# Attention of a two-layer diffusion transformer on one core: transposes and values issued in longer runs, three engines in an order written by hand, and a feed-forward entry without GpSimd

## The chip, the core and the metric

The kernel runs on one core of a Trainium2 chip. The metric is the device time of one execution in microseconds (us). Each engine of the core takes its instructions in the order in which they stand in its queue: PE (TensorE) multiplies matrices and transposes, DVE (VectorE) and ACT (ScalarE) do elementwise work and read PE's results out of PSUM, POOL (GpSimd) does elementwise work in SBUF, SP (SyncE) issues most DMAs. They wait for each other through semaphores.

## What is computed

Two post-norm layers over 1024 latent tokens with a prefix of 256 context tokens, model width 1024, all in float32. Layer 0 has two kinds of attention beside each other, layer 1 has one; each layer ends with a convolutional feed-forward network (FFN). Cut to what matters here:

```python
# layer 0, head group A: 8 query heads, 2 key heads, every latent query reads all 1280 keys
p = jax.nn.softmax(gqa_scores(q, k_all), axis=-1); y = gqa_out(p, v_all)
# layer 0, head group B: 8 heads, a neighbourhood of the grid with a bias, plus 256 context keys
p = jax.nn.softmax(jnp.concatenate([s_nb + bias, s_ctx], -1), axis=-1)
# layer 1: 16 query heads, 2 key heads, window of +-128 tokens, 256 context keys, one sink logit per head
p = jax.nn.softmax(jnp.concatenate([s_loc, s_ctx, sink_q], -1), axis=-1)
# every layer
x = layer_norm(ALPHA * x + gate * (y @ w_out), g, b)
f = (silu(conv(h @ w_up)[gate half]) * conv(h @ w_up)[value half]) @ w_down
x = layer_norm(ALPHA * x + gate * f, g, b)
```

## The kernel before

The program is one straight line without loops on the chip: projections of layer 0 (to about 316 us of the span), attention A (316 to 590), attention B (590 to 708), output projection, FFN of the context, FFN of the latents (to about 1650), projections of layer 1, attention C (1824 to 2067), output projection, FFN of layer 1 (from about 2170 to the end).

**A unit of attention.** Scores are computed for one block of 128 queries at a time. `qk_pair` (L911) multiplies q and k in float32r, three products for each of two heads, which PE runs on two halves of its rows; they land in a PSUM tile S of two banks, of which there are two buffers. DVE reads S, negates it, adds mask or bias and finds the row's minimum in the same instruction (L1177 and L1160 in A, L1315 and L1295 in B, L2947 in C; a further small one, L1182, joins two minima in A). `smax1` then has ACT compute the exponential with its sum (L934), DVE the reciprocal of the sum (L936), and POOL the product with it (L937). The result P has to be transposed for the product with v: PE transposes blocks of 128x128 against an identity (L1044 in layer 0, L1009 in layer 1), four to a PSUM bank T, of which there are three buffers; ACT or DVE copies a full bank to SBUF as PT (`evict`, L918, L922, L924); PE multiplies PT with v into the PSUM tile pv (L1058, L1018). In the profile each of these matmuls with v counts as two. One such bank, from its transposes to its products with v, is what the code calls a bank; its products are a closure called `late`.

**What sets the order.** `pipeline` walks over a list of slices. Each slice computes the scores of one unit (A takes three slices for a block of four heads: context keys, then the latent keys of two heads, then of the other two; B takes one slice for two heads of a block; C takes two slices of two heads). After the scores of a slice it issues the products with v of the banks that were transposed in the slice before (`flush`), and then transposes some more banks from a queue (`take`). On PE the order of each slice is therefore scores, values, transposes. The context manager `manual_pe` keeps the order in which the code is written for PE alone; the instructions of ACT, DVE, POOL and SP are placed by a scheduler of the compiler layer.

**Buffers.** The tile pv has one buffer of a PSUM bank, written anew for each block. P has 8 buffers in layer 0 and 12 in layer 1, PT 9 and 10. The queries of A are loaded into a pool of their own (`aq`, three buffers). Weights of the large products are split into a high and a low float32r part and kept in a ring of 12 SBUF buffers (`ring`).

**Work that goes along.** During B the first rows of the output weight are loaded into P buffers and split (`out_weight`, `split_out`, L1388 and L1389: a cast on ACT, a subtraction on DVE); in C it is the same with four pieces, and x is loaded, scaled and stored in eight groups (`x_load`, `x_scale`, L2890 to L2893).

**The entry of layer 1's FFN.** The last block of tokens runs through LayerNorm, is transposed and modulated (`build_B1`) and split into high and low parts (L1796, L1797). The sums of a Strassen scheme, tiles T0 to T3, are split in the same way by `make` (L1911 on ACT, L1912 on DVE or POOL), in three pieces each. Then PE's products L1879 of the first pair of FFN columns follow, in the order T1, T0, T2, T3. The subtraction of the last block's h3lb and the first, large piece of T0, T2 and T3 stand on POOL.

Of the kernel before, what the change touches and what calls it, by code (L numbers as in the profile page):

```python
# [29 lines left out]
NEG = -1e30  # L30
ORDER = [f + h for f in range(NF // 4) for h in (0, NF // 4)]
# [6 lines left out]
class Kern:  # L38
# [476 lines left out]
    def l0_project(self):  # L515
# [311 lines left out]
        self.aq = eA.enter_context(self.pool("aq", bufs=3))  # L827
# [64 lines left out]
    def load_q(self, qp, src):  # L892

        q = self.t(qp, [128, 2, 2, 256], "q", R)
        for j in range(2):
            self.nc.sync.dma_start(f32(q[:, j]), src[j])
        return q
# [28 lines left out]
    def smax1(self, sp, P, n, negm, nsink=None):  # L926

        nc = self.nc
        den = self.t(sp, [128, 1], "den", bufs=6)
        m = n  # L930
        if nsink is not None:
            nc.gpsimd.tensor_copy(P[:, n : n + 1], nsink)
            m = n + 1
        nc.scalar.activation(P[:, :m], P[:, :m], AF.Exp, bias=negm, scale=-1.0, accum_out=den)  # L934
        rin = self.t(sp, [128, 1], "rin", bufs=6)
        nc.vector.reciprocal(rin, den)  # L936
        nc.gpsimd.tensor_scalar(P[:, :n], P[:, :n], rin, 1.0, ALU.mult, ALU.mult)  # L937

    def pipeline(self, slices):

        fifo, late, pend = [], [], []

        def flush(n):
            done = False
            while len(late) > n and not (done and late[0][0]):
                done = late[0][1]  # L950
                late.pop(0)[3]()

        def take(pop, chunk, keep):
            flush(keep)
            n = 0
            while fifo and pop > 0:
                if n >= chunk:
                    flush(keep)
                    n = 0
                w, first, last, bank = fifo.pop(0)  # L960
                while sum(x[2] for x in late) + w > 9:
                    late.pop(0)[3]()
                late.append((first, last, w, bank()))
                pop -= w
                n += w

        for loads, unit, pop, banks, chunk, keep, *delay in slices:
            for ld in loads:
                ld()
            unit()  # L970
            take(pop, chunk, keep)
            fifo += pend
            pend = []
            if delay:
                pend = banks()
            else:
                fifo += banks()
# [2351 lines left out]
```

## Time and profile before

| | |
|---|---|
| time, median of 3 runs | 2816.75 us (2812.15 to 2818.3) |
| the profiled execution | 2817.18 us, span 2815.3 us |
| mean granted TensorE clock | 0.992 |
| busy share of the span | PE 97%, weight loads 80%, DVE 76%, ACT 49%, POOL 23% |
| chain that ended last | PE 70%, issue 10%, DVE 9%, DMA 4%, ACT 3%, POOL 2% |

The span is the time from the first to the last instruction; the execution takes 1.9 us more. A row of the timeline gives the start in us from the span's start, the duration of the merged group, engine, line, operation, names, shape, the number of instructions and in brackets the idle time of the engine before it with what ended it. The duration of a group of matmuls reaches to the modelled end of its last one; how long a group holds PE is read from its start to the start of the next group. A busy PE need not be at its peak.

### The profile page before, as it was taken

To read this page: it belongs to the slowest core of one execution; us is meant where nothing else is said; L and a number is where in the kernel's file an instruction comes from. 1 tells how busy PE (TensorE), PEld (TensorE's weight loads), DVE (VectorE), ACT (ScalarE), POOL (GpSimd) and SP (SyncE) were. 2 spreads that over 40 slices of the span, in tenths; PEclk is the share of its full clock that TensorE was granted. 3 is DMA by queue.
4 is the path that set the end of the run, shared out by engine and by line. 5 is a ranking of instruction groups with operands and counts; after the bars stand their busy time and mean duration, and the time that the engine had idled before them with its cause. 6 is when DMAs were issued, how large, how long until landed. Compare 5 with 4: busy or idle time off the path is not lost.

```text
span 2815.3 us, 45394 instructions
## 1 busy us (share of the span) xinstructions
PE 2739.8 (97%) x16724; PEld 2245.4 (80%) x16724; DVE 2147.6 (76%) x3867; ACT 1381.5 (49%) x2596; POOL 657.7 (23%) x953
## 2 busy tenths in 40 slices
PE   8999899999999999999999999999999999999998
PEld 6877677878889988888888888766677788888887
DVE  4886476776688778888877656677778888888878
ACT  4321355577336654555553344167754455455542
POOL 3601233355440000000001002255534111111002
PEclk9999999999999999999999999999999999999999
DMA  7669601042658653343367525652245355455962
GB/s 272 192 206 291 199 28 35 11 164 91 186 161 256 206 158 105 113 122 110 117 222 275 179 98 169 205 163 79 90 130 187 119 175 178 161 172 202 341 231 97
DMA packets 369349, 457.01 MB, mean 162 GB/s; under 512 B 26008, under 2 KB 265016, under 8 KB 367592
## 3 DMA queue, kind: packets, MB, share of 16 engines
q1 hardware_dynamic: 341512, 369.27, 41.2%
q0 software_dynamic: 24576, 82.89, 8.6%
q8 instruction: 131, 2.15, 0.3%
q10 hardware_dynamic: 3040, 1.97, 0.2%
q14 instruction: 90, 0.74, 0.1%
HBM read 338.11 MB, written 115.93 MB: 161 GB/s over the span
## 4 chain that ended last, share of the span: by engine, by line
PE 70%; issue 10%; DVE 9%; DMA 4%; ACT 3%; POOL 2%; SPq 0%; ACTq 0%; DVEq 0%; POOLq 0%
PE q L1879 7%; PE x L1879 7%; PE y L1879 6%; PE S L911 5%; PE dy L2585 4%; PE T L1044 4%; PE pv L1058 4%; PE mm L430 3%; PE v L1879 3%; PE mm L432 3%; PE mm L431 3%; PE dx L2585 3%; PE d L431 3%; PE d L432 3%; PE d L430 3%
## 5 line engine op out<-in xcount | busy, mean ns | idle before, releaser
L937 POOL TENSOR_SCALAR P<-P,rin 128x640 f32<-128x640 f32 (+3 forms) x288 | 252.1, 882 | 306.3 <-DVE rin L936 275.5
L1853 DVE TENSOR_TENSOR w<-raw,w 128x512 fp32r<-128x512 f32 x308 | 207.4, 687 | 84.1 <-ACT w L1851 83.7
L112 ACT CAST w<-raw 128x512 fp32r<-128x512 f32 x315 | 183.4, 621 | 167.9 <-PE d L432 64.6
L113 DVE TENSOR_TENSOR w<-raw,w 128x512 fp32r<-128x512 f32 x315 | 206.0, 695 | 69.5 <-ACT w L112 67.5
L911 PE MATMUL S<-k,q 64*128 64x256 f32 (+2 forms) x1824 | 198.4, 340 | 11.4 <-DVE nm L2947 4.4
L934 ACT ACTIVATE P<-P,nm 128x641 f32<-128x641 f32 (+4 forms) x208 | 161.4, 777 | 86.1 <-DVE nm L2947 46.4
L1851 ACT CAST w<-raw 128x512 fp32r<-128x512 f32 x308 | 182.2, 620 | 22.6 <-DVE raw L1858 11.3
L911 PEld LDWEIGHTS S<-k,q 64*128 64x128 f32 x1824 | 139.3, 190 | 49.6 <-issue 16.0
L1044 PE MATMUL T<-ident,P 128*128 128x128 f32 x1008 | 136.7, 283 | 12.0 <-POOL P L937 4.7
L430 PE MATMUL d<-w,w 128*128 128x512 f32 x352 | 137.5, 391 | 0.0
L432 PE MATMUL d<-w,w 128*128 128x512 f32 x352 | 137.0, 389 | 0.0
L431 PE MATMUL d<-w,w 128*128 128x512 f32 x352 | 137.0, 389 | 0.0
L1044 PEld LDWEIGHTS T<-ident,P 128*128 128x128 f32 x1008 | 110.5, 143 | 32.2 <-issue 17.9
L1058 PE MATMUL pv<-PT,v 128*64 128x128 f32 x2016 | 131.8, 279 | 3.7 <-ACT PT L924 2.5
L1058 PEld LDWEIGHTS pv<-PT,v 128*64 128x64 f32 x2016 | 109.0, 137 | 28.5 <-issue 13.5
L1879 PE MATMUL q<-T3h,w 128*128 128x512 f32 x352 | 118.7, 399 | 9.1 <-DVE ug L2539 7.1
L934 ACT ACTIVATE P<-P,mc 128x1280 f32<-128x1280 f32 (+1 forms) x80 | 94.7, 1188 | 64.5 <-DVE mc L1182 62.5
L936 DVE RECIPROCAL rin<-den 128x1 f32<-128x1 f32 x288 | 46.2, 161 | 100.1 <-ACT P L934 98.3
L2585 PE MATMUL dy<-w,w 128*128 128x512 f32 x528 | 120.8, 390 | 0.4 <-DVE w L113 0.4
L1879 PE MATMUL q<-T2h,w 128*128 128x512 f32 x352 | 115.8, 390 | 0.9 <-ACT q L2101 0.9
L2585 PEld LDWEIGHTS dy<-w,w 128*128 128x128 f32 x528 | 99.0, 188 | 21.8 <-DVE w L113 0.8
L1879 PE MATMUL y<-T1h,w 128*128 128x512 f32 x352 | 115.5, 389 | 0.0
(468 smaller groups left out, 7792.6 us busy)
## 6 DMA issues: line engine op xcount, KB each, us to landing
raw<-in_up_dram SPq DMA_DIRECT2D x132, 512.0 KB
raw<-in_down_dram SPq DMA_DIRECT2D x59, 512.0 KB
raw<-g SPq DMA_DIRECT2D x44, 512.0 KB
raw<-G SPq DMA_DIRECT2D x38, 512.0 KB
araw<-in_ada_w_dram SPq DMA_DIRECT2D x32, 512.0 KB
raw<-in_w_in_dram SPq DMA_DIRECT2D x28, 512.0 KB
g<-cv POOLq DMA_DIRECT2D x22, 512.0 KB, 3.0
G<-go POOLq DMA_DIRECT2D x44, 256.0 KB, 3.0
```

The lines of the kernel that those rows point to most:

```text
L113: (lo_eng or nc.vector).tensor_sub(lo, s, f32(hi))
L430: nc.tensor.matmul(ps, lh, rh, start=first, stop=False)
L431: nc.tensor.matmul(ps, lh, rl, start=False, stop=False)
L432: nc.tensor.matmul(ps, ll, rh, start=False, stop=last)
L911: self.nc.tensor.matmul(outs[a], q[r, x, qs], k[r, y, ks], start=(i == 0), stop=(i == 2))
L934: nc.scalar.activation(P[:, :m], P[:, :m], AF.Exp, bias=negm, scale=-1.0, accum_out=den)
L937: nc.gpsimd.tensor_scalar(P[:, :n], P[:, :n], rin, 1.0, ALU.mult, ALU.mult)
L1044: nc.tensor.transpose(ps[:, s * 128 : (s + 1) * 128], P[a][:, cols[i + x] : cols[i + x] + 128], self.ident,)
L1058: nc.tensor.matmul(O[a * HD : (a + 1) * HD], v_of(a, vts[i + x]), pT[:, s * 128 : (s + 1) * 128], start=(i + x == 0), stop=(i + x == m - 1 ...
L1853: nc.vector.tensor_sub(half(i, 1), src[i], f32(half(i, 0)))
L1879: nc.tensor.matmul(ps, w[:, a, s], r[b][:, k], start=first and k + i == 0, stop=k == 3 and i == 2, skip_group_check=True,)
L2585: nc.tensor.matmul(banks[q][t], ga[i][:, a, c], wd[i][:, b], start=q < 2 and f + k == 0, stop=f == HF - 1 and k == 2, skip_group_check=True,)
```

## The change

**Order.** `pipeline` is rewritten. A unit now returns its DVE reductions and its exponentials as two lists instead of issuing them. For each slice the code says how many banks to transpose and how many waiting products with v to keep back, so that a slice either transposes (up to ten banks in a row) or multiplies with v, not both. The new context manager `manual_all` fixes the written order on PE, ACT and DVE; POOL and SP stay with the scheduler. Reciprocals of one slice's sums are placed between the reductions of the next slice. In a slice that transposes, the exponentials stand behind the copies of the transposed banks; in one that does not, they stand ahead of the products with v. Which of ACT and DVE copies a bank out is a fixed string per stage ("AADAD" in C, ENGA in A, "AAA" and "DDA" by turns in B; A is ACT, D is DVE).

**Buffers.** The tile pv is allocated once and its two halves are used by turns (`o_half`). P in layer 0 has 7 buffers, and A has 4 of its own beside them; PT has 10; the queries of A are loaded into the ring. The small y tiles have 2 buffers where they had 3.

**Splits.** The output weight's pieces and the first block of the attention's result are split one slice (B) or one group (C) after their load is issued. The scaling of x follows one group after its load. In the FFN of the context, the split of the first row of the down weight moves from the end of the output projection into the first turn of the loop.

**FFN entry of layer 1.** The four subtractions on POOL move to DVE.

```diff
+ENGA = ("ADADA", "AADAD")
...
+        for loads, unit, keep, pop, banks in slices:
             for ld in loads:
                 ld()
-            unit()
-            take(pop, chunk, keep)
-            fifo += pend
...
+            reds, exps = unit()
+            for i, red in enumerate(reds):
+                red()
+                for f in fins[i * len(fins) // len(reds) : (i + 1) * len(fins) // len(reds)]:
+                    f()
+            n = min(max(pop(len(fifo)), 0), cap)
+            if not n:
+                fins = [e() for e in exps]
+            if keep is not None:
+                flush(keep)
+            flush(max(cap - n, 0))
+            for _ in range(n):
+                late.append(fifo.pop(0)())
+            if n:
+                fins = [e() for e in exps]
+            fifo += banks()
...
+    def o_half(self, O):
+        self.noh = getattr(self, "noh", -1) + 1
+        return O[:, self.noh % 2 * 256 : self.noh % 2 * 256 + 256]
...
+    def manual_all(self):
+        E = mybir.EngineType
+        return self.tc.manual_schedule(engines={E.PE, E.Activation, E.DVE})
...
-                        (ctx_part, 2, lambda: [], 4, 1),
-                        (lambda: lat_part(0), 5, lambda: banks(0), 5, 1),
-                        (lambda: lat_part(1), 3, lambda: banks(1), 4, 0),
+                        (ctx_part, 2 if t < 2 else None, (lambda n: 0) if (kv, t) == (0, 0) else (lambda n: n - 5), lambda: []),
+                        (lambda: lat_part(0), 4, (lambda n: n) if (kv, t) == (0, 0) else (lambda n: 0), lambda: banks(0)),
+                        (lambda: lat_part(1), 0, lambda n: 0, lambda: banks(1)),
...
-                        (unit(0), 3, lambda: [], 4, 0), (unit(1), 2, values, 4, 0)
+                        (unit(0), None if one else 0, lambda n: n if one else 0, lambda: []),
+                        (unit(1), 0 if one else None, lambda n: 0 if one else n, values),
...
-            (nc.gpsimd if t == NLAT - 1 else nc.vector).tensor_sub(l, s, f32(h))
+            nc.vector.tensor_sub(l, s, f32(h))
...
                 for m in (1, 0, 2, 3):
-                    make[m](0, eng=nc.gpsimd if m != 1 else None)
-                    make[m](1, 2)
+                    make[m](0, 1, 2)
```

What this does to the order shows best in pieces of the engines' queues. In the names, S is a score tile, T a bank of transposes, PT its copy, pv the product with v; a number behind a name tells tiles apart. PE in attention C before, from the end of one slice's scores to the next slice's transposes:

```order
L911 MATMUL S_19990<-k_18639,q_19711 128x384
L911 MATMUL S_19989<-k_18639,q_19711 128x384
L911 MATMUL S_19990<-k_18639,q_19711 128x384
L1018 MATMUL pv_19092<-PT_19972,v_19267 64x256 x2
L1018 MATMUL pv_19092<-PT_19979,v_19267 64x256 x2
L1018 MATMUL pv_19092<-PT_19986,v_19267 64x256 x2
L1009 MATMUL T_20025<-ident_58,P_19839 128x128
L1009 MATMUL T_20025<-ident_58,P_19897 128x128
```

And now, from the end of a slice's scores to the start of the next:

```order
L914 MATMUL S_19881<-k_18600,q_19660 128x384
L914 MATMUL S_19882<-k_18600,q_19660 128x384
L1023 MATMUL pv_19053<-PT_19844,v_19227 64x256 x2
L1023 MATMUL pv_19053<-PT_19851,v_19227 64x256 x2
L1023 MATMUL pv_19053<-PT_19858,v_19227 64x256 x2
L1023 MATMUL pv_19053<-PT_19865,v_19227 64x256 x2
L914 MATMUL S_19922<-k_18600,q_19660 128x256
L914 MATMUL S_19923<-k_18600,q_19660 128x256
```

Before, three (or two) banks' products with v stand between the scores and two or three banks of transposes. Now all the banks of a group stand in one run, and a run of scores follows each run of either kind.

ACT in attention A before; P is the exponential, den its sum, PT<-T the copy of a bank:

```order
L934 ACTIVATE P_4531,den_4660<-P_4531,mc_4527 128x1280
L934 ACTIVATE P_4532,den_4667<-P_4532,mc_4527 128x1280
L918 COPY PT_4718<-T_4713 128x512
L918 COPY PT_4767<-T_4762 128x512
L918 COPY PT_4810<-T_4805 128x512
L918 COPY PT_4817<-T_4812 128x512
L934 ACTIVATE P_4725,den_4785<-P_4725,mc_4723 128x1280
L934 ACTIVATE P_4726,den_4792<-P_4726,mc_4723 128x1280
L918 COPY PT_4838<-T_4833 128x512
L934 ACTIVATE P_4727,den_4856<-P_4727,mc_4723 128x1280
L934 ACTIVATE P_4728,den_4863<-P_4728,mc_4723 128x1280
```

And now, over one block of four heads:

```order
L921 COPY PT_4470<-T_4465 128x512
L921 COPY PT_4477<-T_4472 128x512
L921 COPY PT_4491<-T_4486 128x512
L921 COPY PT_4505<-T_4500 128x512
L921 COPY PT_4519<-T_4514 128x512
L921 COPY PT_4533<-T_4528 128x512
L938 ACTIVATE P_4438,den_4553<-P_4438,mc_4436 128x1280
L938 ACTIVATE P_4439,den_4555<-P_4439,mc_4436 128x1280
L938 ACTIVATE P_4440,den_4608<-P_4440,mc_4436 128x1280
L938 ACTIVATE P_4441,den_4610<-P_4441,mc_4436 128x1280
```

The copies stood between the exponentials, one to four at a time; now six copies follow each other, and the four exponentials of the block stand together ahead of the next six.

DVE at the entry of layer 1's FFN before, where the large pieces of T0, T2 and T3 and h3lbl are missing since they stand on POOL:

```order
L1812 TENSOR_TENSOR w_23606<-hst_23589,b_23480 128x512
L1796 CAST h3lbh_22676<-hst_23599 128x4x128
L1813 TENSOR_TENSOR w_23606<-hst_23599,w_23606 128x512
L1814 TENSOR_TENSOR w_23607<-hst_23599,hst_23589 128x512
L1815 TENSOR_TENSOR w_23607<-b_23492,w_23606 128x512
L1912 TENSOR_TENSOR T1l_23659<-gk_23660,T1h_23658 128x2x4x128
L1912 TENSOR_TENSOR T1l_23659<-go_23657,T1h_23658 128x4x128
L1912 TENSOR_TENSOR T1l_23659<-w_23606,T1h_23658 128x4x128
L1912 TENSOR_TENSOR T0l_23655<-go_23657,T0h_23654 128x4x128
L1912 TENSOR_TENSOR T0l_23655<-w_23606,T0h_23654 128x4x128
L1912 TENSOR_TENSOR T2l_23662<-ua_23664,T2h_23661 128x4x128
L1912 TENSOR_TENSOR T2l_23662<-w_23607,T2h_23661 128x4x128
```

And now:

```order
L1853 TENSOR_TENSOR w_23567<-hst_23550,b_23441 128x512
L1837 CAST h3lbh_22637<-hst_23560 128x4x128
L1854 TENSOR_TENSOR w_23567<-hst_23560,w_23567 128x512
L1838 TENSOR_TENSOR h3lbl_22638<-hst_23560,h3lbh_22637 128x4x128
L1855 TENSOR_TENSOR w_23568<-hst_23560,hst_23550 128x512
L1856 TENSOR_TENSOR w_23568<-b_23453,w_23567 128x512
L1953 TENSOR_TENSOR T1l_23620<-gk_23621,T1h_23619 128x2x4x128
L1953 TENSOR_TENSOR T1l_23620<-go_23618,T1h_23619 128x4x128
L1953 TENSOR_TENSOR T1l_23620<-w_23567,T1h_23619 128x4x128
L1953 TENSOR_TENSOR T0l_23616<-ua_23617,T0h_23615 128x2x4x128
L1953 TENSOR_TENSOR T0l_23616<-go_23618,T0h_23615 128x4x128
L1953 TENSOR_TENSOR T0l_23616<-w_23567,T0h_23615 128x4x128
```

Four subtractions have joined the queue, h3lbl among the sums and the others each ahead of its tile's smaller pieces; T1 stands where it stood but for h3lbl.

233 lines of the change are left out of this document (126 added, 107 removed).

## Prediction

> **What bounds the kernel now.** I read the page first, then the stages in the table of windows, then PE's timeline inside each stage, and last the waits of the engines that feed it. The page has PE busy for 97% of the span:
>
> ```profile
> PE 2739.8 (97%) x16724; PEld 2245.4 (80%) x16724; DVE 2147.6 (76%) x3867; ACT 1381.5 (49%) x2596; POOL 657.7 (23%) x953
> ```
>
> So whatever is gained comes either from the 75 us (2815.3 less 2739.8) in which PE stands idle, or from busy time that is no work. The windows tell where the idle time lies. The columns are the stretch, its length, the busy time of PE, PEld, DVE, ACT and POOL, the granted clock, and the DMA share with GB/s. The rows are attention A, attention B, attention C, and 50 us at the entry of layer 1's FFN:
>
> ```profile
> 316.00:590.00 274.00, 260.31 (x2796) 210.93 (x2797) 192.06 (x580) 153.00 (x276) 108.78 (x118) 0.98 0.18 57
> 590.00:708.00 118.00, 111.75 (x1284) 91.69 (x1284) 80.94 (x245) 87.58 (x219) 64.18 (x81) 0.99 0.35 119
> 1824.00:2067.00 243.00, 230.81 (x1994) 159.22 (x1991) 177.67 (x475) 167.61 (x390) 128.37 (x266) 0.98 0.36 108
> 2160.00:2210.00 50.00, 42.95 (x182) 33.92 (x181) 41.86 (x56) 23.83 (x39) 16.41 (x9) 0.97 0.40 123
> ```
>
> In these 685 us PE is idle for 13.7, 6.3, 12.2 and 7.1 us. DVE is busy for 70, 69 and 73% of the three attention stages and ACT for 56, 74 and 69%: no engine but PE is near its limit on the average, but they feed PE in bursts. The rest of the program does not change, so 39 us of idle time are at stake, and beside them whatever PE's busy time hides. One period of A (a block of four heads) shows that:
>
> ```profile
> 405.37 2.53 PE L1044 MATMUL T<-ident,P 128*128 128x128 f32 x20
> 407.83 1.65 PE L911 MATMUL S<-k,q 64*128 64x512 f32 x12
> 409.42 2.84 PE L1058 MATMUL pv<-PT,v 128*64 128x128 f32 x48
> 412.19 1.53 PE L1044 MATMUL T<-ident,P 128*128 128x128 f32 x12
> 413.65 0.97 PE L911 MATMUL S<-k,q 64*128 64x256 f32 x12
> 414.55 1.09 PE L1058 MATMUL pv<-PT,v 128*64 128x128 f32 x16
> 415.58 1.09 PE L1044 MATMUL T<-ident,P 128*128 128x128 f32 x8
> 416.60 2.08 PE L911 MATMUL S<-k,q 64*128 64x512 f32 x12
> 418.61 1.09 PE L1058 MATMUL pv<-PT,v 128*64 128x128 f32 x16
> 419.64 0.55 PE L1044 MATMUL T<-ident,P 128*128 128x128 f32 x3
> ```
>
> From start to start, two banks of pv (x16) hold PE for 1.03 us and x48 for 2.77, that is 0.0544 us each; 16 of them alone would be 0.87, so 0.16 us belong to the run and not to its matmuls. Transposes: x8 take 1.02 and x12 1.46, 0.11 each, and 0.14 belong to the run. Runs of pv and transposes thus cost 0.15 us apiece before they do anything. The period, from one x20 to the next, is 14.27 us. In C the runs are as short:
>
> ```profile
> 1843.78 0.98 PE L911 MATMUL S<-k,q 64*128 64x256 f32 x12
> 1844.68 1.52 PE L1018 MATMUL pv<-PT,v 128*64 128x256 f32 x12
> 1846.13 1.09 PE L1009 MATMUL T<-ident,P 128*128 128x128 f32 x8
> 1847.15 1.15 PE L911 MATMUL S<-k,q 64*128 64x256 f32 x12
> 1848.23 1.08 PE L1018 MATMUL pv<-PT,v 128*64 128x256 f32 x8
> 1849.25 1.53 PE L1009 MATMUL T<-ident,P 128*128 128x128 f32 x12
> 1850.71 1.15 PE L911 MATMUL S<-k,q 64*128 64x256 f32 x12
> ```
>
> Here x12 and x8 of pv take 1.45 and 1.02 (0.108 each, 0.16 over), x8 and x12 transposes 1.02 and 1.46: the same 0.15. This block takes 6.93 us.
>
> **The change, part by part.**
>
> *Fewer runs.* Counted in the order of both kernels, layer 0 has 177 runs of transposes and pv before and 92 now, layer 1 has 126 and 64; the runs of scores stay. 147 runs fewer at 0.15 us are 22 us. The new order has borders that the rows above lack, scores to transposes and pv to scores. The three kinds of border that they show cost about the same, so I take 0.15 for these too; the bounds are nothing (a further gain of 0.15 for each of the 71 runs of transposes, 11 us) and twice that (a loss of 11 us). The Trainium skill, "TensorEngine Tiling (Array Packing)", section Key Properties, says that changing the tiling mode drains the array; scores, transposes and pv use 64x128, 128x128 and 128x64 of it, so by that rule each of the new borders drains too, and the sum stays at 22 us.
>
> *Attention A: longer bursts against three PSUM banks.* What fed PE in small pieces now comes at once: ten banks are transposed in a row, and only three fit into PSUM. These rows price what must happen between:
>
> ```profile
> 406.12 1.07 ACT L918 COPY PT<-T 128x512 f32<-128x512 f32 x2 [2.97 <-PE T L1044]
> 406.94 1.29 DVE L918 COPY PT<-T 128x512 f32<-128x512 f32 x2
> 412.54 1.36 ACT L934 ACTIVATE P<-P,mc 128x1280 f32<-128x1280 f32 x1 [2.18 <-DVE mc L1182]
> 418.49 1.23 DVE L1177 TENSOR_SCALAR_CACHE_REDUCE P<-S 128x1024 f32<-128x1024 f32 x1 [0.92 <-PE S L911]
> ```
>
> A copy on ACT starts 0.75 us after the first transpose of its bank (406.12 against 405.37) and copies follow each other at about 0.52; DVE's take 0.65. The exponential of 1280 takes 1.36, a reduction of 1024 on DVE 1.23, and the reduction starts 0.1 us before the next run on PE does (418.49 against 418.61). Set 0 at the end of the last scores of a block. PE multiplies with v until 1.9, computes the context scores until 2.8 and starts its 40 transposes. DVE's two reductions, with the small operations between, end at 1.1 and 2.5; ACT's exponentials, which stand ahead of the copies in its queue, end at 2.7 and 4.1. Three banks are full at 4.1; the first copy ends at 4.7, so PE waits 0.6 us. Then a buffer returns about every 0.47 us against 0.44 for four transposes, which adds 0.2. The burst ends at 8.0 and the rest, scores of 1.59, pv x48 of 2.77 and scores of 1.59, needs no further wait, since the reductions of the first of them end at 12.1 and PE comes to the second at 12.5. The new period is 1.9 + 0.9 + 4.5 + 0.8 + 1.6 + 2.8 + 1.6 = 14.1 against 14.27. Three runs fewer save 0.45 and the waits ahead of pv go, and the burst gives most of it back. Over 16 blocks that is 3 us. Had the exponentials ended 0.7 later (one reduction waiting for a reciprocal), it would be +0.5 per block, 8 us lost; with no wait at all in the burst, -1.0 per block, 16 us won.
>
> *Attention B.* 18 slices lie between these two scores, 3.46 us each:
>
> ```profile
> 635.29 0.98 PE L911 MATMUL S<-k,q 64*128 64x256 f32 x12
> ...
> 697.58 0.98 PE L911 MATMUL S<-k,q 64*128 64x256 f32 x12
> ...
> DVE w L1389 <- ACT w L1388: 5.4, 4, 3.8
> ```
>
> Two slices lose two runs, 0.3 us, and six banks in a row wait for a buffer by the reasoning above for about 0.2: 0.1 us over 18 pairs, 2 us. At its beginning DVE waited four times, 5.4 us in all, in the split of the output weight (last row). The split now follows a slice (3.4 us) after its load, and its load has to wait for a P buffer, of which there are 7 instead of 8; I take 4 us of the 5.4, with 0 and 5.4 as bounds. Together 6 us.
>
> *Attention C.* Between these rows lie 18 blocks of 7.54 us:
>
> ```profile
> 1884.38 0.38 PE L911 MATMUL S<-k,q 64*128 64x256 f32 x1 [0.36 <-DVE nm L2947]
> ...
> 2020.11 1.15 PE L911 MATMUL S<-k,q 64*128 64x256 f32 x12
> ...
> PEld pv L1018 <- ACT PT L924: 21.4, 57, 1.0
> ...
> L934 ACT ACTIVATE P<-P,nm 128x641 f32<-128x641 f32 (+4 forms) x208 | 161.4, 777 | 86.1 <-DVE nm L2947 46.4
> ...
> L2947 DVE CUSTOM_DVE_ANT_0 P<-S,msk,snk 128x640 f32<-128x640 f32 (+1 forms) x128 | 103.6, 845 | 10.7 <-PE S L911 10.3
> ```
>
> The third row says that weight loads of pv waited 57 times for a copy, 21.4 us in all; the last two have the mean of an exponential (0.78) and of a reduction (0.85). In the new order the five banks of a block are transposed, then scores are computed, and only then multiplied with v: the scores (1.08 us) cover the last copy. Of a burst of five banks the fourth starts when the first copy ends, 0.75 + 0.61 after the start against 1.31 of work: a wait of 0.1. Runs of this kind give 2 x 1.08 for scores, 2.33 each for pv and for transposes (x20), and 0.1: 6.9 us. ACT's three copies and four exponentials take 1.6 + 3.1, DVE's four reductions and two copies 3.4 + 1.3, so neither is late; the scaling of x (two operations of 0.7 on DVE in eight blocks) now stands in a fixed place, ahead of a reduction, and I add 0.15 for it. 18 x 0.49 is 9 us; the 13 blocks at both ends, where waits were fewer, give 0.4 each, 5 us. Together 14 us, of which 9 are runs. The bounds are 5 (the waits stay) and 22.
>
> *Entry of layer 1's FFN.* These are three of PE's waits, two of DVE's subtractions of 512 elements, and one of POOL's of 1024:
>
> ```profile
> 2176.60 2.36 POOL L1912 TENSOR_TENSOR T0l<-ua,T0h 128x1024 fp32r<-128x1024 f32 x1
> 2176.67 2.84 DVE L1912 TENSOR_TENSOR T2l<-ua,T2h 128x512 fp32r<-128x512 f32 x1 [1.19 <-POOL h3lbl L1797]
> 2179.02 0.50 PE L1879 MATMUL v<-T0l,w 128*128 128x512 f32 x1 [1.64 <-POOL T0l L1912]
> 2185.04 0.68 DVE L1912 TENSOR_TENSOR T3l<-w,T3h 128x512 fp32r<-128x512 f32 x1
> ...
> 2189.84 0.50 PE L1879 MATMUL q<-T3h,w 128*128 128x512 f32 x1 [1.92 <-DVE ug L2539]
> 2206.41 0.79 PE L1879 MATMUL q<-T3h,w 128*128 128x512 f32 x1 [2.65 <-DVE ug L2539]
> ```
>
> While POOL works, DVE needs 2.84 us for what takes 0.68 once POOL is done (2185.04). Three such subtractions on DVE cost 6.5 us more than they have to. On DVE alone the work is h3lbl, 512 elements at 0.6, and three pieces of 1024, at twice that by the same row: 4.2 us added, and 6.5 + 1.2 (its wait for POOL's h3lbl, 2176.67) taken away: DVE comes to its next work 3.5 us earlier. PE's waits of 1.64 and 1.92 go nearly whole, and the first split of T1 comes 0.6 later, which PE feels at once. The later wait for the same chain on DVE (q again, 2.65 us at 2206.41) moves along rather than goes. I take 4 us, between 0 and 5.5.
>
> *At nothing.* The queries in the ring: their loads wait for PE's last use of a weight of the projections, and they are needed when attention starts; a late one would show as a wait of the first scores for a DMA. The halves of pv: a wait for the copy of y goes that was short. The split of the down weight in the context's FFN moves two casts and two subtractions past a wait of PE for ACT; by the 0.68 of such a subtraction it is worth 1.4 us either way.
>
> **The sum.** A 3, B 6, C 14, FFN 4: 27 us off the profiled execution's 2817.18, which is 0.4 above the median of 2816.75. 2790 us.
>
> **The rivals.**
>
> *No wait is left.* If ACT and DVE, free of the scheduler's order, keep up everywhere, A gives 16, B 9, C 22, FFN 5: 52 us, 2765 us. For it speaks that neither is busy for more than three quarters of a stage; against it the three PSUM banks. Chance 0.08.
>
> *The wait only moves.* The 22 us of runs come, but the bursts wait for copies as much as they save, and FFN gives its 4: with A at +8, B at +2, C at -5 and FFN at -4 it is 2818 us. The rows of A, where the price hangs on a margin of half an exponential, speak for it; C's spare time speaks against. It spreads from 2808 to 2822. Chance 0.13.
>
> *Order by hand blocks.* ACT now does its exponentials as a group and its copies as a group, and a reciprocal on DVE that stands between two reductions waits for an exponential that ACT has put behind copies. If each burst finds one exponential more ahead of its first copy than I count, 16 bursts of A pay 1.36 and 17 of B and 31 of C 0.78: 59 us, less the 27 won: 2849 us. It decides from 27/59, 0.46 of an exponential per burst. For it: in my walk through A the exponentials end just when PE's three banks are full, so that any more is paid whole. Against it: in C, the same walk has them end over a us before the first copy is due. The Trainium skill, "PSUM — Partial Sum Buffer", section Engine vs sequencer instructions, calls the queues of ACT and DVE strict FIFO, so that nothing behind a late exponential can pass it; nothing in the old order, where copies and exponentials were interleaved, shows how much that costs here. Chance 0.15.
>
> That the change doesn't do what it says is excluded by the order: the runs are as long as written, and POOL has lost its four subtractions.
>
> **How the numbers follow.** The forecast has 0.64. The range takes in the end with no wait left and the case in which the wait moves, and leaves out the blocked order: 2764 to 2816. A measurement of this kernel can tell about 0.2%, 5.6 us, from no change. Slower by more than that: the blocked order, 0.15. Within it (2811 to 2822): half of the moved wait, 0.07. Faster: the rest, 0.78.
>
> **What would show it.** In the profile after, runs of 20 and 40 transposes with 0.11 us each and 0.15 beside; A's period at 14.1 with a wait of 0.6 to 0.8 inside the 40 transposes; C's at 6.9 without waits of pv for copies; DVE's T2l and T3l at 0.7, and no POOL between. Wrong would be: A's period above 14.6 with ACT's exponentials ahead of waiting copies; the new borders far from 0.15; or waits of the first scores for queries from the ring.

## The result and the profile after

The changed kernel takes 2852.63 us (median of 4 runs, 2847.17 to 2859.8) against 2817.05 for the kernel before: a ratio of 1.0132, 95% interval 1.0115 to 1.0149. It is 36 us slower where 27 us faster was forecast. The profiled execution took 2853.84 us with a span of 2852.1.

The windows table of the kernel after, cut where its stages begin and end (attention A, attention B, attention C, 50 us at the entry of layer 1's FFN; columns as in the prediction):

```profile
316.00:584.80 268.80, 229.66 (x2470) 187.02 (x2468) 172.05 (x511) 148.41 (x250) 95.67 (x104) 0.97 0.13 43
584.80:767.00 182.20, 147.75 (x1620) 123.75 (x1620) 95.50 (x300) 105.96 (x263) 76.72 (x101) 0.93 0.29 99
1880.00:2110.00 230.00, 218.47 (x1989) 162.40 (x1989) 166.76 (x470) 171.86 (x395) 129.49 (x266) 0.98 0.37 114
2201.00:2251.00 50.00, 46.19 (x206) 37.32 (x205) 42.33 (x66) 26.43 (x44) 2.44 (x5) 1.00 0.45 141
```

PE is now idle for 39.1 us in the first window and 34.5 in the second, where A and B together had 20.0 before; C is shorter. To see where time went, each matmul outside attention was set against the same one of the kernel before. The distance between the two is +1.7 us when attention A starts, +58.9 when B has ended, +55.4 when C starts, +42.8 when it has ended, +37.5 at 50 us into layer 1's FFN, and +36.7 at the end. So A and B lost 57 us, C won 12.6, the FFN entry 5.3; the 3.5 us won between B and C are taken apart by no run.

What PE waits for in A (two rows) and B (two rows) of the kernel after: sum in us, times, longest.

```profile
PE pv L1063 <- DVE y L1209: 17.9, 16, 2.5
PE T L1049 <- ACT PT L921: 14.2, 15, 2.2
```

```profile
PE pv L1063 <- ACT yb L1345: 28.8, 13, 5.1
PE pv L1063 <- DVE y L1209: 2.1, 2, 1.5
```

The same view of B before has of this kind one line:

```profile
PE pv L1058 <- ACT yb L1328: 0.4, 1, 0.4
```

The wait for a copy of transposes (T) is the one that the prediction walked through. The wait of a product with v (pv) for y or yb, 48.8 us in A and B, was not in its sum. y and yb are the copies of a finished accumulator from PSUM to SBUF, on DVE in A and on ACT in B. One period of A on PE in the kernel after:

```profile
416.73 1.53 PE L1049 MATMUL T<-ident,P 128*128 128x128 f32 x12
419.12 3.48 PE L1049 MATMUL T<-ident,P 128*128 128x128 f32 x28 [0.87 <-ACT PT L921]
422.54 1.66 PE L914 MATMUL S<-k,w 64*128 64x512 f32 x12
424.13 2.40 PE L1063 MATMUL pv<-PT,v 128*64 128x128 f32 x40
427.40 0.66 PE L1063 MATMUL pv<-PT,v 128*64 128x128 f32 x8 [0.86 <-DVE y L1209]
427.98 1.67 PE L914 MATMUL S<-k,w 64*128 64x512 f32 x12
...
432.38 1.53 PE L1049 MATMUL T<-ident,P 128*128 128x128 f32 x12
```

And DVE at the same time (L1189 reduces scores; this is the second of two reductions):

```profile
425.58 1.22 DVE L1189 TENSOR_SCALAR_CACHE_REDUCE P<-S 128x1024 f32<-128x1024 f32 x1
...
426.92 0.42 DVE L1209 COPY y<-pv 128x256 f32<-128x256 f32 x1
```

The run of 48 pv is 40 of one accumulator, the last five banks of a block of heads, and 8 of the next. PE is through with the 40 at about 426.3. DVE is then still at its second reduction and copies y from 426.92 to 427.34; PE goes on at 427.40. The period is 15.65 us.

In B it is worse, since ACT makes the copy and has exponentials ahead of it. PE and ACT of the kernel after:

```profile
617.40 1.31 PE L1063 MATMUL pv<-PT,v 128*64 128x128 f32 x20
620.50 1.31 PE L1063 MATMUL pv<-PT,v 128*64 128x128 f32 x20 [1.78 <-ACT yb L1345]
...
626.35 1.31 PE L1063 MATMUL pv<-PT,v 128*64 128x128 f32 x20
```

```profile
618.45 0.83 ACT L938 ACTIVATE P<-P,nm 128x640 f32<-128x640 f32 x1
...
619.28 0.81 ACT L938 ACTIVATE P<-P,nm 128x640 f32<-128x640 f32 x1
...
620.09 0.35 ACT L1345 COPY yb<-pv 128x256 f32<-128x256 f32 x1
```

The first 20 pv finish an accumulator, the next 20 begin another. Between them ACT does two exponentials and only then makes yb. This pair of slices takes 8.95 us (617.40 to 626.35) where one took 6.92 on the mean. Stretches at half clock (a granted clock of 0.5; 16 pv take 1.98 us instead of 1.09) follow many of the longer waits: A and B have 44.4 us of them, before 17.1.

The three longest of these waits, 3.76, 4.14 and 5.08 us, have one thing more in them, the split of an output weight. Here is the first of them on PE, on DVE and on ACT:

```profile
639.88 1.98 PE L1063 MATMUL pv<-PT,v 128*64 128x128 f32 x16 [3.76 <-ACT yb L1345]
```

```profile
636.02 1.29 DVE L1419 TENSOR_TENSOR w<-P,w 128x512 fp32r<-128x512 f32 x2 [1.17 <-ACT w L1418]
```

```profile
638.02 0.72 ACT L938 ACTIVATE P<-P,nm 128x512 f32<-128x512 f32 x1 [1.51 <-DVE rin L942]
```

DVE waits for ACT's casts of the weight and subtracts, and its reductions of the scores stand behind that; ACT's exponentials wait for the reductions, and yb stands behind the exponentials. These three waits are 13 of B's 28.8 us. The split has a fixed place in this order because it was written there.

Not every pair of slices waits so. A pair of heads has nine slices and the runs follow pairs of slices, so in the second and fourth pair of heads the runs begin where accumulators begin, and in the first and third one slice off. But for one of 0.47 us at 611, the waits for yb lie between 617 and 666 and between 695 and 746; between 667 and 694, and from 747 on, there is none.

C and the FFN entry went as forecast. A block of C in the kernel after takes 6.87 us (1946.75 to 1953.62):

```profile
1946.75 2.48 PE L1014 MATMUL T<-ident,P 128*128 128x128 f32 x20
...
1950.24 2.38 PE L1023 MATMUL pv<-PT,v 128*64 128x256 f32 x20
1952.55 1.14 PE L914 MATMUL S<-k,q 64*128 64x256 f32 x12
1953.62 2.49 PE L1014 MATMUL T<-ident,P 128*128 128x128 f32 x20
```

At the FFN entry DVE's subtractions run at their own pace, and one wait of PE for them is left. The later wait for the chain on DVE stays as it was, 2.66 us at 2245.33 where it was 2.65, as the prediction had it:

```profile
2223.94 0.69 DVE L1953 TENSOR_TENSOR T3l<-w,T3h 128x512 fp32r<-128x512 f32 x1
```

```profile
2217.66 0.50 PE L1920 MATMUL y<-T1l,w 128*128 128x512 f32 x1 [1.01 <-DVE T1l L1953]
```

### The profile page after: what moved, and what is told of

Same layout as the page of the kernel before. It is cut to its first block, busy times and chain, and to the rows that moved or that the text cites. A ratio compares the mean times of both kernels' runs of the same rounds, so it can differ in the third digit from the quotient of the medians.

```text
span 2852.1 us, 45421 instructions
## 1 busy us (share of the span) xinstructions
PE 2727.2 (96%) x16724; PEld 2252.4 (79%) x16724; DVE 2125.5 (75%) x3849; ACT 1399.1 (49%) x2618; POOL 642.1 (23%) x949
## 4 chain that ended last, share of the span: by engine, by line
PE 73%; issue 10%; DVE 9%; ACT 4%; DMA 2%; POOL 2%; SPq 0%; ACTq 0%; DVEq 0%; POOLq 0%
PE q L1920 7%; PE x L1920 7%; PE y L1920 7%; PE S L914 5%; PE dy L2625 4%; PE T L1049 4%; PE mm L431 4%; PE mm L433 4%; PE mm L432 3%; PE v L1920 3%; PE dx L2625 3%; PE d L431 3%; PE d L433 3%; PE d L432 3%; PE pv L1063 3%
## 5 line engine op out<-in xcount | busy, mean ns | idle before, releaser
L921 ACT COPY PT<-T 128x512 f32<-128x512 f32 (+1 forms) x256 | 137.2, 568 | 119.3 <-PE T L1049 83.6
L1063 PE MATMUL pv<-PT,v 128*64 128x128 f32 x2016 | 137.0, 288 | 48.7 <-ACT yb L1345 28.8
L1063 PEld LDWEIGHTS pv<-PT,v 128*64 128x64 f32 x2016 | 115.5, 143 | 72.0 <-ACT yb L1345 32.1
L1049 PE MATMUL T<-ident,P 128*128 128x128 f32 x1008 | 132.4, 283 | 19.2 <-ACT PT L921 15.8
L2995 DVE CUSTOM_DVE_ANT_0 P<-S,msk,snk 128x640 f32<-128x640 f32 (+1 forms) x128 | 107.5, 841 | 46.2 <-PE S L914 44.8
L921 DVE COPY PT<-T 128x512 f32<-128x512 f32 x160 | 108.0, 685 | 39.7 <-PE T L1049 32.3
L1189 DVE TENSOR_SCALAR_CACHE_REDUCE P<-S 128x1024 f32<-128x1024 f32 x64 | 77.9, 1218 | 66.4 <-PE S L914 66.4
L914 PE MATMUL S<-k,q 64*128 64x256 f32 (+1 forms) x1200 | 118.0, 324 | 9.4 <-DVE nm L2995 7.3
```

The costliest lines, as they stand in the source:

```text
L914: self.nc.tensor.matmul(outs[a], q[r, x, qs], k[r, y, ks], start=(i == 0), stop=(i == 2))
L921: return (self.nc.vector.tensor_copy if eng == "D" else self.nc.scalar.copy)(dst, src)
L1049: nc.tensor.transpose(ps[:, s * 128 : (s + 1) * 128], P[a][:, cols[i + x] : cols[i + x] + 128], self.ident,)
L1063: nc.tensor.matmul(O[a * HD : (a + 1) * HD], v_of(a, vts[i + x]), pT[:, s * 128 : (s + 1) * 128], start=(i + x == 0), stop=(i + x == m - 1 ...
```

## A tally that closes

For A and B, the time from the start of each run on PE to the start of the next was taken, less a fixed price for each matmul in the run (0.109 us a transpose, 0.0546 a pv, 0.059, 0.0875 or 0.1165 a score matmul of 256, 384 or 512 columns). All kernels below compute the same matmuls, so the differences do not hang on these prices. What is left are the runs' own costs, the waits and the half clock. In us, with the number of runs (the last one is not counted), and as the last column the length of A and B together, from the first score to the last pv:

| kernel | scores | transposes | pv | sum | A and B |
|---|---|---|---|---|---|
| before | 34.2 (87) | 31.8 (88) | 17.8 (88) | 83.8 | 392.5 |
| after | 30.8 (86) | 38.3 (39) | 71.9 (52) | 141.0 | 449.6 |
| ends between runs | 33.8 (86) | 29.0 (39) | 28.5 (52) | 91.3 | 399.9 |
| copies first | 36.4 (86) | 38.4 (39) | 34.5 (52) | 109.3 | 418.0 |
| two accumulator banks | 30.0 (86) | 86.0 (39) | 15.4 (52) | 131.4 | 440.1 |
| A and B of before | 34.3 (87) | 30.6 (88) | 16.7 (88) | 81.6 | 390.3 |
| more ends | 36.8 (86) | 25.5 (39) | 24.7 (52) | 87.1 | 395.8 |
| reductions later | 38.5 (86) | 32.0 (39) | 26.2 (52) | 96.7 | 405.3 |
| order by the scheduler | 27.0 (86) | 58.5 (39) | 51.3 (52) | 136.9 | 445.6 |
| no inner ends | 42.9 (86) | 26.9 (39) | 13.5 (54) | 83.4 | 392.0 |

From before to after the sum rises by 57.2: pv +54.1, transposes +6.5, scores -3.4. It is the pv.

## The experiments

Three theories. Theory 1: a run of pv that finishes one accumulator and begins another must wait inside itself for the copy of the first. Theory 2, the prediction's rivals: the long bursts of transposes against three PSUM banks, with exponentials ahead of the copies. Theory 3: the accumulator's bank is the limit, whatever stands ahead of the copy.

### Ends between runs

The runs of pv are cut where accumulators end; nothing is done to the copies.

```diff
-                        (lambda: lat_part(0), 4, ...
+                        (lambda: lat_part(0), 5, ...
...
-            for i, gs in enumerate([[8, 9]] + [[g] for g in range(NLAT)]):
+            lat = [[g] for g in range(NLAT)]
+            for i, gs in enumerate(lat + [[8, 9]] if j % 2 == 0 else [[8, 9]] + lat):
...
-                        if len(out) == 1 else (None, lambda n: n - 3) if len(out) % 2
+                        if len(out) == 1 else (None, lambda n, w=nb[-1]: n - w) if len(out) % 2
```

Here nb[-1] is the number of banks of the slice before.

> Edit: in attentions A and B the runs of pv end where an accumulator is finished (A: five banks and five instead of six and four; B: heads 0 and 2 take their context queries last, and the transposes stop at a slice's end), so that no run of pv begins a second accumulator. Order of ACT and DVE as in the changed kernel. Theory 1 (the loss is PE waiting inside a run of pv for the copy of the accumulator just finished, 17.9 us in A and 30.9 in B, and the half clock that follows long waits): both waits go, since scores and transposes lie between; A's period falls from 15.65 to about 14.6; 2797 to 2808 us. Theory 2 (the long bursts of transposes against three PSUM banks, with exponentials ahead of the copies, are what costs): the wait only moves to the transposes, 2845 to 2855 us.

Measured: 2803.99 us (2801.14 to 2804.96) against 2818.83 for the kernel before, ratio 0.9947 (0.9932 to 0.9961). PE's waits in A and B:

```profile
PE pv L1063 <- DVE y L1209: 8.7, 5, 2.5
PE pv L1063 <- ACT yb L1345: 5.8, 2, 3.8
PE T L1049 <- ACT PT L921: 5.4, 15, 0.6
```

The waits for y and yb fall from 48.8 us to 14.5, and those for copies of transposes fall too, from 15.8 to 5.4, instead of taking their place. A pair of slices in B now reads:

```profile
597.54 2.71 PE L1049 MATMUL T<-ident,P 128*128 128x128 f32 x20
...
601.09 2.40 PE L1063 MATMUL pv<-PT,v 128*64 128x128 f32 x40
...
604.32 2.53 PE L1049 MATMUL T<-ident,P 128*128 128x128 f32 x18
```

The order of exponentials and copies on ACT and DVE is what it was, and 49 us are back. Theory 1 said 2797 to 2808, theory 2 at least 2845. Six of the seven waits left are at accumulators of the context queries, which have only two banks (16 pv), so that an accumulator still ends inside a run; the seventh, 0.53 us, is at the end of A.

### The copies ahead of what stood ahead of them

PE's order is that of the changed kernel; the pv, and the copies that follow them, are issued earlier.

```diff
             for i, red in enumerate(reds):
+                if not n and i == 1:
+                    drain()
                 red()
...
-            if not n:
-                fins = [e() for e in exps]
...
-            if n:
-                fins = [e() for e in exps]
+            fins = [e() for e in exps]
```

> Edit: PE's order unchanged; where a slice transposes nothing, the pv of late banks, and with it the copy of a finished accumulator, is issued after the first reduction of the slice and before its exponentials, so that ACT's copy yb stands ahead of two exponentials and DVE's copy y ahead of the second reduction. Theory 1: the wait in A falls from 0.86 to about 0.4 a block (7 us less), those in B from 1.7 to about 0.4 (20 us less, and some half clock): 2815 to 2828 us. Theory 2 (bursts of transposes): the bursts are as they were, 2847 to 2857 us. Theory 3 (the accumulator's bank is the limit, whatever stands ahead of its copy): the waits stay above 0.8, 2845 us or more.

Measured: 2836.88 us (2832.94 to 2842.04), ratio 1.0066 (1.0051 to 1.0081).

```profile
PE T L1053 <- ACT PT L921: 15.4, 24, 1.1
PE pv L1067 <- DVE y L1213: 10.3, 18, 0.8
PE pv L1067 <- ACT yb L1349: 6.8, 13, 0.7
```

The waits for y and yb fall to 17.1 us, 0.53 and 0.47 each time, and A and B take 418.0 us instead of 449.6, as theory 1 asked. But the total gained only 16 us and lies in none of the three ranges. One reason is an effect that the edit did not intend: `pipeline` also runs C, where ACT's exponentials now come after the pv and just ahead of the copies of transposes. There 20 transposes hold PE for 2.65 us (1924.00 to 1926.65 in this run's profile) where they held it for 2.41, and 9.3 us of C's gain go (the distance to the kernel before falls by 3.3 us over C, by 12.6 in the changed kernel). What A and B say goes against theory 3 too: what stands ahead of the copy sets the length of the wait, though not whether there is one.

### Two banks for accumulators

```diff
-            pt = es.enter_context(self.pool("aTp", bufs=3, space=PSUM))
-            po = es.enter_context(self.pool("aO", bufs=1, space=PSUM))
-            po = self.t(po, [128, 512], "pv")
+            pt = es.enter_context(self.pool("aTp", bufs=2, space=PSUM))
+            po = es.enter_context(self.pool("aO", bufs=2, space=PSUM))
...
-                    box["O"] = self.o_half(po)
+                    box["O"] = self.t(po, [128, 512], "pv")
```

> Edit: accumulators of A and B alternate between two PSUM banks instead of two halves of one; the transposes have two banks instead of three. Theory 1 with the bank as the object of the wait: no pv waits for y or yb any more (49 us of waits gone), but a bank of transposes returns only every 0.65 us instead of 0.47, so the bursts wait more: about 2 us a block in A (35 us) and 0.8 a pair in B (14 us): 2840 to 2870 us, with all PE waits on PT copies. If the halves already were independent and the wait has another cause, pv still waits for y and yb as before: 2890 or more.

Measured: 2840.55 us (2839.99 to 2844.61), ratio 1.0081 (1.0066 to 1.0096).

```profile
PE T L1049 <- ACT PT L921: 27.2, 36, 2.3
PE T L1049 <- DVE PT L921: 17.1, 48, 1.9
...
PE pv L1063 <- DVE y L1208: 2.4, 3, 0.9
PE pv L1063 <- ACT yb L1344: 1.6, 1, 1.6
```

With a bank for each accumulator the waits for y and yb are 4.0 us, although their copies stand where they stood and PE's order is the same. So the two halves of one bank, which the change uses by turns, do not free PE from the copy: the program makes it wait until the copy has read its half. The Trainium skill, "PSUM — Partial Sum Buffer", section "PSUM bank collisions raise a hardware error", says that the compiler orders any two instructions of different engines that touch the same bank in the same quadrant of partitions, also at different columns of it; the waits here, present with halves and gone with banks, agree. Each accumulator has not only a bank but also a tile of its own in this run, so it does not show which of the two the program orders by. The price is the transposes' third bank: their waits rise from 15.8 to 44.3 us, and the tally for transposes from 38.3 to 86.0.

### A and B of before, the rest of after

The old `pipeline`, `groups_a`, `slices_b` and their helpers serve A and B, the new ones C; everything else is as in the changed kernel.

> Edit: attentions A and B with the pipeline, the order of ACT and DVE by the scheduler, the query buffers and the value accumulators of the kernel before; attention C, FFN entry and the rest as in the changed kernel. If the stages add up independently (A and B lost 57 us, C won 12.6, the FFN entry and what follows 6): 2796 to 2801 us, faster than both. Should C or the entry depend on what A and B leave (ring buffers, clock), 2805 or more.

Measured: 2797.72 us (2795.93 to 2802.88), ratio 0.9932 (0.9915 to 0.9949). The stages add up: in this run's profile 12.4 us are won over C and 4.6 behind it, without the new A and B; the other 4.8 lie ahead of C.

### More ends between runs

```diff
-            while len(late) > n:
+            done = False
+            while len(late) > n and not (stop and done and late[0].first):
+                done = late[0].last
                 late.pop(0)()
```

> Edit: as the run with run ends, and in A the pv that follow the first latent scores also stop where an accumulator is finished around the context queries (five places, where that run still waited 1.7 to 2.5 us for y). Theory 1 (a run of pv that begins a second accumulator waits for the copy of the first): these five waits, 8.7 us, go but for the last at A's end (0.5), two of the half-clock stretches too: 2793 to 2798 us. Theory 2 (what is left in A is the transposes' wait, and the wait moves there): 2802 to 2806 us.

Measured: 2804.15 us (2802.73 to 2804.87), ratio 0.9948 (0.9933 to 0.9962): the same as without this edit. The time lies in the range of theory 2, but not for its reason: the waits for copies of transposes are 4.8 us, where they were 5.4. The expectation counted wrongly. Of the five places two lost their wait and one, 0.53 us at the end of A, was meant to stay. In the other two the context's accumulator ended in the next run instead, and that run waits 2.26 us.

```profile
PE pv L1066 <- ACT yb L1349: 5.9, 2, 3.9
PE pv L1066 <- DVE y L1213: 5.0, 3, 2.3
PE S L914 <- DVE P L1193: 4.9, 8, 0.8
```

The third row has grown: scores wait for the reductions on DVE eight times, 4.9 us in all and up to 0.8 each, where they had waited twice, 1.1 us in all. In the profile A and B are 4.1 us shorter, but the projections ahead of them were 3.4 us longer in this execution, and the medians do not show a gain.

### Reductions behind the first copies

```diff
+            k = 3 if n == cap and not exps else 0
+            if k:
+                for f in fins:
+                    f()
...
+                for _ in range(k):
+                    late.append(fifo.pop(0)())
             for i, red in enumerate(reds):
```

> Edit: as the run before it, and in A's bursts of 40 transposes DVE makes its copies of the first three banks before the four reductions of the context's scores (1.7 us) instead of behind them. ACT's order is unchanged. If DVE's reductions hold up the burst, its wait of 0.4 to 0.6 a block goes: 5 to 8 us less than that run. If ACT's exponentials (two of 1.36 ahead of its first copy) hold it up, no change within 2 us.

Measured: 2813.21 us (2810.71 to 2820.47), ratio 0.9986 (0.9976 to 0.9996): 9 us slower than the run before it, which neither side expected. A's period rises from 14.28 to 14.65 us. Waits inside the bursts come more often, 24 times instead of 14, with 6.0 us in all instead of 4.8, and in the profiled execution A and B have 23.9 us at half clock instead of 10.2. Which instruction makes them late was not pursued; that moving DVE's reductions away helps is refuted.

### Order by the scheduler

```diff
-            with self.manual_all():
+            with self.manual_pe():
                 self.pipeline(self.slices(ga) + sb)
```

> Edit: PE's order of A and B as in the changed kernel; ACT and DVE there ordered by the scheduler, as before the change. If the place of the accumulators' copies in ACT's and DVE's hand-written order is the cause (behind exponentials and reductions), the scheduler puts them earlier: 2815 to 2838 us. If PE's order alone is the cause (a run that begins a second accumulator in the same bank must wait, whatever the other engines do): 2847 to 2857 us.

Measured: 2854.79 us (2851.08 to 2859.66), ratio 1.0134 (1.0114 to 1.0154), as the changed kernel.

```profile
PE T L1049 <- ACT PT L921: 33.3, 23, 2.4
PE pv L1063 <- ACT yb L1345: 18.0, 13, 2.2
PE pv L1063 <- DVE y L1209: 16.8, 18, 1.9
```

Left to the scheduler, ACT and DVE make PE wait 34.8 us for y and yb instead of 48.8, and 33.3 for transposes instead of 15.8. No wait for yb is longer than 2.2 us now, where those with the split in them took up to 5.1. The order by hand is thus no worse than the scheduler's for this order of PE as a whole: it loses 14 us at the accumulators' copies and wins 17.5 in the bursts. The loss comes with the order of PE.

### The FFN entry alone

The kernel before, with nothing changed but these lines:

```diff
-            (nc.gpsimd if t == NLAT - 1 else nc.vector).tensor_sub(l, s, f32(h))
+            nc.vector.tensor_sub(l, s, f32(h))
...
-                    make[m](0, eng=nc.gpsimd if m != 1 else None)
-                    make[m](1, 2)
+                    make[m](0, 1, 2)
```

> Edit: the kernel before with the entry of layer 1's FFN alone changed (POOL's four subtractions on DVE, each query part in one piece). If POOL and DVE slowed each other there, DVE's subtractions of 512 take 0.7 us instead of 2.8 and 4 to 5 us go: 2813 to 2815 us. If the gain in the changed kernel at this place came from an earlier arrival and not from this edit: no change, 2817 to 2819 us.

Measured: 2811.42 us (2807.94 to 2815.01, 8 runs) against 2817.62, ratio 0.9975 (0.9964 to 0.9987), a little more than expected. The distance to the kernel before falls by 5.3 us over the entry, as in the changed kernel. The Trainium skill, "SBUF — State Buffer", section "SBUF: two separate sides", has DVE and GpSimd share a pair of ports, which one holds for a whole instruction while the other stands still; of DVE's instructions that concerns, among others, those with two inputs in SBUF, beside one of GpSimd that reads SBUF. These subtractions have two such inputs, and DVE's 2.84 us beside POOL and 0.69 without it agree.

### No end inside a run

```diff
-                        (lambda: lat_part(1), 0, lambda n: 0, lambda: banks(1)),
+                        (lambda: lat_part(1), -0.5, lambda n: 0, lambda: banks(1)),
...
-                        else (0, lambda n: 0)
+                        else (-0.25 if len(out) in (12, 30) else 0, lambda n: 0)
```

A negative number asks for the stop at a finished accumulator; -0.25 has the exponentials follow the pv instead.

> Edit: as the run with all ends, and the last inner ends go too: the pv behind the second latent scores stop at a finished accumulator as well (the two places that still waited 2.26 us for y), and in the two slices of B whose run holds the context queries of two heads ACT makes the copy yb ahead of the two exponentials (waits of 3.9 and 2.0 us). Theory 1 (waits of runs that begin a second accumulator): 10 us of waits less, some half clock with them: 2790 to 2797 us. If other waits take their place (scores waiting for the reductions behind y, seen in the run before): 2800 to 2805 us.

Measured: 2794.82 us (2793.54 to 2798.43) against 2819.93, ratio 0.9917 (0.9895 to 0.9938): the fastest of all, 25 us under the kernel before and 58 under the changed one.

```profile
PE S L914 <- DVE P L1193: 5.0, 8, 0.8
...
PE pv L1066 <- DVE y L1213: 3.0, 3, 1.2
PE pv L1066 <- ACT yb L1349: 0.9, 2, 0.5
```

The waits for y and yb are 3.9 us. The pv in A and B cost 13.5 us beyond their matmuls, less than the 17.8 before the change. But A and B as a whole only come back to 392.0 us, where they were 392.5, because the scores cost more. So the new order wins nothing in A and B even now; in this run's profile 17.8 us are won from C's start on. These are the two runs of latent scores of a block in A on PE, and DVE's second reduction between them:

```profile
429.95 1.66 PE L914 MATMUL S<-k,w 64*128 64x512 f32 x12
431.54 2.40 PE L1066 MATMUL pv<-PT,v 128*64 128x128 f32 x40
433.87 2.05 PE L914 MATMUL S<-k,w 64*128 64x512 f32 x12
435.85 2.40 PE L1066 MATMUL pv<-PT,v 128*64 128x128 f32 x40
```

```profile
432.99 1.22 DVE L1193 TENSOR_SCALAR_CACHE_REDUCE P<-S 128x1024 f32<-128x1024 f32 x1
```

The first run holds PE for 1.59 us, the second for 1.98. It begins at 433.87, while DVE still reads the second of the two score tiles, until 434.2; there are only two. Its second matmul starts at 434.27, 0.4 us after the first.

## Why the prediction was wrong

- **At nothing (the step that failed).** "The halves of pv: a wait for the copy of y goes that was short." The step took the two halves of the bank for two buffers and did not ask where in the new runs an accumulator ends. The copy reads one half while the next pv write the other, and PE waits for it all the same. The old `flush` had a rule for that: it stopped when an accumulator was finished and another came next (`not (done and late[0][0])`, in the code before). The new one has none, and so the wait did not go: it grew from 0.4 us in B to 48.8 in A and B, and 27 us more at half clock came with it. Shown by the runs with ends between runs (49 us back), with two banks (the waits gone) and with no inner ends (58 us back). The rows that price it stood in the trace of before: two reductions of 1.23 us, or two exponentials of 0.78, now stand in the same slice ahead of the copy. Of the other items at nothing, the queries in the ring held: no score in A waits for a DMA.
- **Fewer runs.** 0.15 a run held, the new borders included: in C of the kernel after, pv to scores costs 0.15, and runs of scores cost 0.19 to 0.20 ahead of transposes as ahead of pv. The Trainium skill, "TensorEngine Tiling (Array Packing)", section Key Properties, on which the prediction drew, says that changing the tiling mode drains the array; that the new borders cost as much as the old ones agrees.
- **Attention A.** Forecast 14.1 us a period with 0.8 of wait in the burst; it was 15.65, of which the run of 48 pv has 1.05 more than forecast (3.85 against 2.8) and the burst 0.5 more (5.81 against 5.3). Without inner ends the period is 14.3, against 14.27 before: the burst of 40 gives back what three runs fewer save. The walk had PE come to the second latent scores at 12.5, 0.4 after the reductions; with 40 pv instead of 48 it comes 0.44 sooner, and waits. So of the 3 us forecast nothing is left even then.
- **Attention B.** Forecast 6 us won. In the run with ends between runs the pair shown takes 6.78 us (597.54 to 604.32), the one before it 6.95 (590.59 to 597.54), against 6.92 before; without inner ends B's tally is 29.0 us against 30.9. So 2 us, not 6.
- **Attention C.** Forecast 14 us, 6.9 us a block: 12.6 and 6.87.
- **FFN entry.** Forecast 4 us between 0 and 5.5: 5.3 at the place, and DVE's subtractions at the 0.7 forecast.
- **The rivals.** "Order by hand blocks" gave 2849 us with a chance of 0.15, and the time came near. That was luck, for its mechanism is not what cost the time: it put one exponential more ahead of the copies of transposes in each burst, and the waits for these copies came to 15.8 us in all, where the walk had allowed for about 0.8 a block. Nor is the order by hand to blame for the loss as a whole, since the scheduler's takes as long; what it does cost is the split in three of B's waits. That the slow side deserved more than 0.15 follows from what was left out: every long run was checked for what it has to read, and not for the buffer that it writes.

Left open: the scores of A without inner ends cost 10 us more than before (31.6 against 21.6 in the tally), and the 0.4 us a block shown above make up some 6 of them over 16 blocks; where the rest goes, and why the reductions behind the first copies cost 9 us, was not settled.

## What to carry to other kernels

When runs are made longer, mark in the new order where each accumulator ends: an end inside a run costs the whole wait for its copy, with all that stands ahead of the copy on the copying engine, and an end between runs costs little as long as enough other work follows (48.8 us of waits became 3.9). Two halves of one PSUM bank were one buffer here, since one engine wrote and another read. And a change that loses may hold parts that win: without the new A and B the kernel takes 2797.72 us against 2818.83, and 17 us of the gain lie in C and behind it.

## What the runs showed of the hardware

Half clock can follow waits of 2.5 us: with the wait of 2.54 us at 459.9 in the kernel after come 3.4 us at half clock, with that of 2.44 us at 695.4 come 6.8 us, while after one of 2.18 us at 481.7 there are none. The length of the wait alone does not settle it: in the kernel before, 3.4 us at half clock begin at 608.6, behind a wait of 1.54 us that ended at 606.55. Such a wait costs more than its own length. The other surprise is how little the bursts' wait cost once the pv no longer waited: in the run with more ends it fell from 0.87 us to between 0.2 and 0.33 in most blocks of A, with the bursts as they were. Part of that is time: eight pv (0.44 us) moved from ahead of the second latent scores to behind them, so PE comes to the burst that much later after these scores.
